# Copying the diagonal blocks of a 64x64 triangular inverse on GpSimd instead of ScalarE, in a one-core RWKV-7 / RetNet inference step

## The chip, the core and the metric

The kernel runs on one core of a Trainium2 chip. The metric is the device time of one execution in microseconds (us); the number that counts is the median of several runs. The profile comes from one more execution of the same program.

The engines are called here as the profile calls them: PE (TensorE, matmuls; PEld is its weight load), DVE (VectorE), ACT (ScalarE), POOL (GpSimd) and SP (which only issues transfers). Each engine works through its own list of instructions strictly in order, so an instruction that waits holds back everything behind it on that engine.

## What is computed

The reference is one step of a two-layer decoder over 256 prompt tokens and 8 single-token samples, which the kernel treats as one matrix of 264 columns. Layer 0 mixes with RWKV-7, layer 1 with RetNet; each layer has a gated feed-forward block ahead of and behind its mixer. The change lies in RWKV-7:

```python
def step(S, inp):                      # one token, per head; S is 64 x 64
    r_t, d_t, k_t, v_t, kk_t, a_t = inp
    sa = jnp.einsum('bhvk,bhk->bhv', S, -kk_t)
    S = (S * d_t[:, :, None, :] + sa[..., None] * (kk_t * a_t)[:, :, None, :]
         + v_t[..., None] * k_t[:, :, None, :])
    return S, jnp.einsum('bhvk,bhk->bhv', S, r_t)
```

## The kernel before

The 256 prompt tokens are taken in four chunks of 64, for 16 heads, two heads to a group of 128 partitions (`f` = 0 to 7). Inside a chunk the recurrence is a unit lower triangular system of 64x64 for each head and chunk. `inverse()` inverts all 64 of them at once, in blocks of 32: DVE inverts the diagonal blocks by back substitution (62 short operations `tm<-V,A` and `V<-V,tm`), transposes them into `Xd` (which lies in `tm`) and transposes half of them again into `AT`. The diagonal blocks are then copied to their places in the result `X`, and the off-diagonal block comes from two rounds of 32x32 matmuls, `ps<-tm,AT` and `ps<-V,AT`, each in two halves with an ACT copy out of PSUM between.

What uses `X` is `heads2(p)`, p = 0 to 3, for two groups each. In its order on PE: `al,ka` and `pp,ka`; `PI,be` and `pp,be` (DVE then takes `M` out of PSUM); `cst,al`; `PI,ka` and `cst,vt` (needs the value rows `vt` of its groups); `VK,KQ`; `z,X` and `aT,X` (needs `X`); `bT,WT` and `M,WT`; a long run of `VK`, `WT,bT`, `KQ,VK`, `M,WT` (called the sums below); three times `G,Ls` and `Ly,G`, with a DVE addition `G<-ps,G` after each; then the head norm `Y,cst`, `sq,cst`, `rd,cst`. `decode()` treats the 8 samples beside it: two times `dS,kkr` on states `dS` that POOL loads, each followed by an ACT copy `yd<-ps` and a matmul `cst,yd`.

The main line of work beside these is the value projection: 8 matmuls `ps<-xv,raw` for each `f`, after which ACT takes the value row out (`vt<-ps`, in `values`). These `xv` matmuls are PE's filler between the short matmuls. Their weights are read straight from the transfer's buffer `raw`. Behind them come the weights of the gate and of the output projection, which are split in two parts instead: ACT writes `hi` from `raw` (L90) and DVE writes `lo` from both (L105), which frees the buffer. There are three `raw` buffers in all, and SP loads the next unit into a buffer as soon as it is free.

The order of instructions is not written by hand. `weave` runs the main line and the side generators against a planner's clock: each operation that goes through a helper (`self.act`, `self.tt`, `self.mm`) adds its planned cost to its engine's clock by `spent`, and side work is let in when the clock says that its inputs are ready. An instruction recorded directly on `nc.gpsimd` adds nothing. Every matmul has line L138, every activation L90, most DVE operations L105.

Of the kernel before, what the change touches and what calls it, by code (L numbers as in the profile page):

```python
# [41 lines left out]
class Step:  # L42
# [158 lines left out]
    def mark(self, key):  # L201
        self.done[key] = self.now
# [242 lines left out]
class Rwkv(Step):  # L445
# [19 lines left out]
    def rwkv(self, gain):  # L465
        nc, tc, ps_, late = self.nc, self.tc, self.ps, self.late
# [5 lines left out]
        with ExitStack() as ctx:  # L472
# [33 lines left out]
            X = P1.tile([128, 32, 64], F32, name="X")  # L506
# [33 lines left out]
            def stream():  # L540
# [26 lines left out]
                for g in range(2):  # L567
                    kp = [ps_()[:, 0:T] for _ in range(4)]
                    for k in range(KT):
                        yield f"mix{k}"  # L570
                        for j in range(4):
                            prod(kp[j], "k", k, 4 * g + j)
                            yield
                    k_out(g, kp)
                self.beside(TU["inverse"], inverse())
                def vs(f):
                    p = ps_()[:, 0:T]
# [219 lines left out]
            def inverse():  # L797
                V, tm = (big(n).rearrange("p (a b) -> p a b", b=32) for n in ("V", "tm"))
                flat32 = lambda t: t.rearrange("p a b -> p (a b)")
                nc.gpsimd.memset(V, 0.0)  # L800
                nc.gpsimd.memset(flat32(V)[:, 0:1024:33], 1.0)
                for f in range(KT):
                    yield f"A{f}"
                self.turn(A3.rearrange("p r s -> p s r"), Ag)
                for m in range(31, 0, -1):
                    n = 32 - m
                    o = tm[:, 0:n, 0:m]
                    self.tt(o, V[:, m:32, m:m + 1].to_broadcast([128, n, m]),
                            A3[:, m:m + 1, 0:m].to_broadcast([128, n, m]))
                    self.tt(V[:, m:32, 0:m], V[:, m:32, 0:m], o, ALU.add)  # L810
                    if TU["INVY"] and m % TU["INVY"] == 0:
                        yield

                Xd = tm
                self.turn(Xd.rearrange("p n i -> p i n"), V)
                mark("W0")
                for e0 in EH:
                    self.turn(AT[e0:e0 + 32], Xd[e0:e0 + 32])
                for e0 in EH:
                    self.act(X[e0 + 32:e0 + 64, :, 32:64], Xd[e0 + 32:e0 + 64])  # L820
                    self.act(X[e0:e0 + 32, :, 0:32], Xd[e0:e0 + 32])
                yield
                for g in range(2):
                    py = ps_().rearrange("p (n s) -> p n s", n=16)
                    for n in range(16):
                        for e0 in EH:
                            hi = slice(e0 + 32, e0 + 64)
                            self.mm(py[e0:e0 + 32, n], AT[hi, 16 * g + n], Xd[hi, 16 * g + n])
                    for e0 in EH:
                        self.act(V[e0:e0 + 32, 16 * g:16 * g + 16], py[e0:e0 + 32])  # L830
                    yield
                for g in range(2):
                    px = ps_().rearrange("p (n s) -> p n s", n=16)
                    for n in range(16):
                        for e0 in EH:
                            lo = slice(e0, e0 + 32)
                            self.mm(px[lo, n], AT[lo, 16 * g + n], V[lo, 16 * g + n])
                    for e0 in EH:
                        self.act(X[e0:e0 + 32, 16 * g:16 * g + 16, 32:64], px[e0:e0 + 32])
                    mark(f"X{g}")  # L840
                    yield
# [758 lines left out]
```

## Time and profile before

| | us |
|---|---|
| three timed runs | 1284.57, 1288.61 (median), 1290.11 |
| the profiled execution | 1283.95 |
| its span, first to last instruction | 1282.2 |
| busy in it: PE, DVE, ACT, POOL | 1254.6, 849.4, 674.1, 68.8 |

The span and 1.75 us around it make the profiled execution's time. PE is busy for 98% of the span, so the time changes when PE is made to wait more or less, and not by what another engine saves for itself. The stretch that the change touches lies at 300 to 420 us.

### The profile page before, as it was taken

How to read it: one execution, taken by the hardware profiler on the slowest of the kernel's cores; microseconds unless marked ns; L12 is line 12 of the kernel's file. 1: busy time of each engine (PE TensorE's matmuls, PEld its weight loads, DVE VectorE, ACT ScalarE, POOL GpSimd, SP SyncE). 2: the span in 40 equal slices, each digit the busy share in tenths (PEclk: the TensorE clock that was granted, in tenths of full speed). 3: DMA queues.
4: the chain of work that ended last, by engine and by line, in shares of the span. 5: the costliest groups of instructions: out<-in, count | busy, mean ns of one | idle time of the engine just before them, and what ended most of it. 6: DMA issues, size and time to landing. Idle time of an engine off the chain costs nothing.

```text
span 1282.2 us, 29100 instructions
## 1 busy us (share of the span) xinstructions
PE 1254.6 (98%) x12194; PEld 1184.4 (92%) x12194; DVE 849.4 (66%) x1391; ACT 674.1 (53%) x1169; POOL 68.8 (5%) x175
## 2 busy tenths in 40 slices
PE   9999999999988999999999999999999999999996
PEld 9999998678777999999999999988888799999996
DVE  6766567589246877766566656677877865766554
ACT  7544442653444777754456454445665554544542
POOL 0000001131200000000000000011111100000000
PEclk9999999999999999999999999999999999999998
DMA  7655554333401566665557555679879655555562
GB/s 236 196 181 181 180 167 140 100 101 117 158 14 43 182 215 216 213 198 181 180 196 264 181 181 181 203 255 348 306 254 329 224 181 180 175 181 180 179 182 83
DMA packets 66755, 239.16 MB, mean 187 GB/s; under 512 B 7504, under 2 KB 8912, under 8 KB 66496
## 3 DMA queue, kind: packets, MB, share of 16 engines
q1 hardware_dynamic: 59472, 212.63, 51.8%
q0 software_dynamic: 6544, 23.40, 4.9%
q8 instruction: 95, 1.56, 0.5%
q10 hardware_dynamic: 608, 1.28, 0.3%
q14 instruction: 36, 0.29, 0.1%
HBM read 214.92 MB, written 22.35 MB: 185 GB/s over the span
## 4 chain that ended last, share of the span: by engine, by line
PE 87%; issue 5%; DMA 3%; DVE 2%; ACT 2%; SPq 0%; DVEq 0%; POOL 0%; ACTq 0%; POOLq 0%
PE ps L138 86%; DMA raw<-in_w 2%; PE ps L153 1%; DVE lo L105 1%; ACT hi L90 1%; DMA dS<-in_wkvt 1%; DMA Sd<-in_wkv 0%; DMA S<-in_ret 0%; ACT L90 0%; DMA out_swkv<-Sd 0%; DVE yl L105 0%; DVE xf L105 0%; DVE on L120 0%; DVE rs L126 0%; ACT sd L90 0%
## 5 line engine op out<-in xcount | busy, mean ns | idle before, releaser
L90 ACT ACTIVATE hi<-raw 128x1024 fp32r<-128x1024 f32 (+1 forms) x344 | 362.6, 1054 | 428.3 <-PE ps L138 210.4
L105 DVE TENSOR_TENSOR lo<-raw,hi 128x1024 fp32r<-128x1024 f32 (+1 forms) x344 | 418.5, 1217 | 229.6 <-ACT hi L90 228.1
L138 PE MATMUL ps<-ah,hi 128*128 128x264 f32 (+1 forms) x1824 | 522.0, 288 | 0.9 <-ACT ah L90 0.8
L138 PE MATMUL ps<-al,hi 128*128 128x264 f32 (+1 forms) x1824 | 515.8, 284 | 0.0
L138 PE MATMUL ps<-ah,lo 128*128 128x264 f32 (+1 forms) x1824 | 513.3, 284 | 0.1
L138 PEld LDWEIGHTS ps<-ah,hi 128*128 128x128 f32 x1824 | 342.0, 188 | 9.2 <-issue 7.4
L138 PEld LDWEIGHTS ps<-al,hi 128*128 128x128 f32 x1824 | 342.7, 188 | 4.1 <-issue 2.9
L138 PEld LDWEIGHTS ps<-ah,lo 128*128 128x128 f32 x1824 | 341.5, 188 | 0.5 <-DVE lo L105 0.3
L138 PE MATMUL ps<-hh,hi 128*128 128x264 f32 x832 | 237.1, 285 | 0.0
L138 PE MATMUL ps<-hl,hi 128*128 128x264 f32 x832 | 237.0, 285 | 0.0
L138 PE MATMUL ps<-hh,lo 128*128 128x264 f32 x832 | 236.8, 285 | 0.0
L138 PEld LDWEIGHTS ps<-hl,hi 128*128 128x128 f32 x832 | 156.8, 188 | 0.0
L138 PEld LDWEIGHTS ps<-hh,lo 128*128 128x128 f32 x832 | 156.7, 188 | 0.0
L138 PEld LDWEIGHTS ps<-hh,hi 128*128 128x128 f32 x832 | 156.4, 188 | 0.1
L105 DVE TENSOR_TENSOR h<-s,ps 128x264 f32<-128x264 f32 x88 | 37.0, 427 | 48.0 <-PE ps L138 46.6
L105 DVE TENSOR_TENSOR t<-ps,rs 128x264 f32<-128x264 f32 x88 | 37.2, 430 | 18.9 <-PE ps L138 18.8
L114 DVE SCALAR_TENSOR_TENSOR S<-ps,ks,S 128x512 f32<-128x512 f32 x64 | 45.0, 742 | 6.2 <-PE ps L138 6.2
L90 ACT ACTIVATE S<-S 128x1024 f32<-128x1024 f32 x32 | 33.7, 1056 | 16.1 <-DMA S<-in_ret 15.9
L90 ACT ACTIVATE hh<-h 128x264 fp32r<-128x264 f32 x88 | 35.3, 409 | 5.8 <-DVE h L105 5.5
L90 ACT ACTIVATE s<-t 128x264 f32<-128x264 f32 x88 | 35.3, 410 | 4.2 <-DVE t L105 4.1
L105 DVE TENSOR_TENSOR hl<-h,hh 128x264 fp32r<-128x264 f32 x88 | 37.0, 427 | 0.4
L90 ACT ACT_TABLE_LOAD x26 | 33.4, 1283 | 2.1 <-PEq L1580 1.7
(265 smaller groups left out, 1196.3 us busy)
## 6 DMA issues: line engine op xcount, KB each, us to landing
raw<-in_w SPq DMA_DIRECT2D x363, 512.0 KB, 3.7
S<-in_ret SPq DMA_DIRECT2D x32, 512.0 KB, 6.1
out_sret<-S POOLq DMA_DIRECT2D x32, 512.0 KB, 3.9
dS<-in_wkvt POOLq DMA_DIRECT2D x4, 512.0 KB, 5.4
Sd<-in_wkv SPq DMA_DIRECT2D x4, 512.0 KB, 5.7
out_swkv<-Sd POOLq DMA_DIRECT2D x4, 512.0 KB, 4.4
out_pret<-so POOLq DMA_DIRECT2D x8, 256.0 KB, 2.3
rcst<-in_rcst SPq DMA_DIRECT2D x1, 1100.0 KB, 6.2
```

What stands on the lines that cost most here:

```text
L90: ins = self.nc.scalar.activation(out=out, in_=in_, func=func, scale=scale, **kw)
L105: ins = self.nc.vector.tensor_tensor(out=out, in0=a, in1=b, op=op)
L114: ins = self.nc.vector.scalar_tensor_tensor(out=out, in0=a, scalar=s, in1=b, op0=op0, op1=op1)
L138: ins = self.nc.tensor.matmul(out=out, lhsT=lhsT, rhs=rhs, start=start, stop=stop)
L153: self.nc.tensor.transpose(out, in_, ident)
```

## The change

Four instructions move from ACT to POOL: the copies of the inverse's diagonal blocks from `Xd` into `X`.

```diff
                 for e0 in EH:
-                    self.act(X[e0 + 32:e0 + 64, :, 32:64], Xd[e0 + 32:e0 + 64])
-                    self.act(X[e0:e0 + 32, :, 0:32], Xd[e0:e0 + 32])
+                    nc.gpsimd.tensor_copy(X[e0 + 32:e0 + 64, :, 32:64], Xd[e0 + 32:e0 + 64])
+                    nc.gpsimd.tensor_copy(X[e0:e0 + 32, :, 0:32], Xd[e0:e0 + 32])
                 yield
```

The copies no longer go through `self.act`, so the planner's ACT clock does not count them, and the order of the whole stretch behind them comes out otherwise. On POOL the four copies stand ahead of the first load of `dS`; up to the place shown next, all engines have the same order as before, but for one exchange of short DVE operations. SP's list is the same. What SP's loads wait for is not.

PE, from about 305 us on (the operands are those named above; `x24` counts equal matmuls in a row; - is before, + is after):

```order
 L138 MATMUL ps<-cst,al 64x64 x24
-L138 MATMUL ps<-xv,raw 128x264 x25
-L138 MATMUL ps<-tm,AT 32x32 x32
-L138 MATMUL ps<-xv,raw 128x264
+L138 MATMUL ps<-xv,raw 128x264 x5
 L138 MATMUL ps<-PI,ka 64x64 x16
 L138 MATMUL ps<-cst,vt 64x64 x16
+L138 MATMUL ps<-xv,raw 128x264 x11
+L138 MATMUL ps<-VK,KQ 64x64 x16
+L138 MATMUL ps<-tm,AT 32x32 x32
+L138 MATMUL ps<-xv,raw 128x264 x3
+L138 MATMUL ps<-tm,AT 32x32 x32
```

Before, 25 `xv` matmuls stand ahead of the inverse's first round; now 16 do, and the first pair of groups has its `PI,ka`, `cst,vt` and `VK,KQ` ahead of it. From `cst,al` to the first `cst,yd` PE has 48 `xv` matmuls before the change and 37 after it, with the same short matmuls; the other 11 now stand later.

ACT, from the first split of a weight unit to the first `yd<-ps` (before):

```order
L90 ACTIVATE hi<-raw 128x1024
L90 ACTIVATE vt<-ps 128x264
L90 ACTIVATE WT<-ps 128x448 x2
L90 ACTIVATE hi<-raw 128x1024
L90 ACTIVATE X<-ps 32x16x32 x2
L90 ACTIVATE hi<-raw 128x1024
L90 ACTIVATE G<-ps 128x256 x2
L90 ACTIVATE Y<-ps 128x256 x2
L90 ACTIVATE yd<-ps 128x64
```

and the same place after:

```order
L90 ACTIVATE hi<-raw 128x1024
L90 ACTIVATE G<-ps 128x256 x2
L90 ACTIVATE Y<-ps 128x256 x2
L90 ACTIVATE hi<-raw 128x1024 x2
L90 ACTIVATE yd<-ps 128x64
```

The second and third `hi` moved behind `G` and `Y`, directly ahead of `yd`. DVE has it alike: its three `lo<-raw,hi` stood apart, ahead of `Ls` and `Ly`; now the three stand together behind `Ls` and `Ly` and directly ahead of the first `G<-ps,G`.

SP, the loads of weights with buffer numbers and the semaphores that each waits for: raw_4300 and the two ahead of it hold `xv` weights, the next three are split (before):

```order
L159 DMA raw_4211<-in_w 128x1024 [waits DMAHW5_49,PE_49]
L159 DMA raw_4300<-in_w 128x1024 [waits DMAHW6_49,PE_49]
L159 DMA raw_4590<-in_w 128x1024 [waits DMAHW7_49,PE_49]
L159 DMA raw_5160<-in_w 128x1024 [waits DMAHW0_49,PE_49]
L159 DMA raw_5509<-in_w 128x1024 [waits DMAHW2_49,DVE_49]
```

and after, where raw_4329 and raw_4799 are the last two units of `xv` weights:

```order
L159 DMA raw_4329<-in_w 128x1024 [waits DMAHW5_49,PE_49]
L159 DMA raw_4799<-in_w 128x1024 [waits DMAHW6_49,PE_49]
L159 DMA raw_5095<-in_w 128x1024 [waits DMAHW7_49,PE_49]
L159 DMA raw_5445<-in_w 128x1024 [waits DMAHW2_49,DVE_49]
L159 DMA raw_5543<-in_w 128x1024 [waits DMAHW3_49,DVE_49]
```

A wait for PE is a wait for the last `xv` matmul on a buffer, a wait for DVE one for a `lo` that frees it. Before, two buffers come free from `xv` matmuls for the units to be split (raw_4590, raw_5160). After, only one does (raw_5095, after the `xv` matmul behind `M,WT`); raw_4329 and raw_4799 keep the other two until `xv` matmuls that stand behind the first `cst,yd`, and so raw_5445 and raw_5543 each wait for the `lo` of the unit ahead of them.

## Rows read from the trace of the kernel before

**Rows 1.** The page: busy time of each engine, its share of the span, its instructions.

```profile
PE 1254.6 (98%) x12194; PEld 1184.4 (92%) x12194; DVE 849.4 (66%) x1391; ACT 674.1 (53%) x1169; POOL 68.8 (5%) x175
```

**Rows 2.** Busy time in stretches of the touched part: length, then busy us (and instructions) of PE, PEld, DVE, ACT and POOL, granted clock, DMA share, GB/s.

```profile
305.00:320.00 15.00, 14.96 (x213) 12.46 (x212) 14.42 (x36) 6.26 (x13) 1.32 (x2) 1.00 0.47 141
320.00:340.00 20.00, 19.95 (x519) 15.92 (x514) 4.82 (x8) 12.65 (x24) 2.83 (x7) 1.00 0.45 146
340.00:350.00 10.00, 7.22 (x314) 6.22 (x308) 1.82 (x7) 1.88 (x7) 3.75 (x9) 0.83 0.41 116
350.00:360.00 10.00, 8.41 (x316) 6.75 (x306) 3.99 (x12) 1.92 (x6) 0.99 (x2) 1.00 0.34 131
360.00:370.00 10.00, 8.89 (x363) 7.47 (x360) 3.40 (x12) 6.51 (x19) 0.00 (x0) 1.00 0.03 5
370.00:380.00 10.00, 9.18 (x265) 7.52 (x259) 6.05 (x19) 4.11 (x15) 0.00 (x0) 1.00 0.02 4
380.00:390.00 10.00, 9.46 (x318) 8.45 (x313) 3.93 (x13) 5.29 (x16) 0.00 (x0) 1.00 0.02 5
390.00:400.00 10.00, 9.19 (x193) 7.33 (x186) 6.81 (x22) 3.51 (x8) 0.00 (x0) 1.00 0.17 54
```

**Rows 3.** The same view in stretches of 1 us, with the same columns.

```profile
343.00:344.00 1.00, 0.20 (x11) 0.04 (x2) 0.00 (x0) 0.00 (x0) 0.00 (x0) 1.00 0.34 131
346.00:347.00 1.00, 1.00 (x7) 0.54 (x6) 0.00 (x0) 0.22 (x1) 0.75 (x1) 0.67 0.00 0
347.00:348.00 1.00, 1.00 (x13) 0.70 (x14) 0.00 (x0) 0.39 (x1) 1.00 (x3) 0.50 0.06 16
348.00:349.00 1.00, 1.00 (x42) 1.00 (x44) 0.36 (x2) 0.00 (x0) 1.00 (x4) 0.50 0.65 82
349.00:350.00 1.00, 1.00 (x56) 1.00 (x52) 0.00 (x0) 0.05 (x1) 1.00 (x4) 0.62 0.85 233
```

**Rows 4.** The view of the DMA queues, from 343 to 344 us: packets, MB, share of 16 engines. Queue q8 brings instructions.

```profile
q8 instruction: 1, 0.02, 5.6%
```

**Rows 5.** PE's waits from 280 to 470 us: what was waited for, us in total, times, longest.

```profile
PE ps L138 <- issue: 4.9, 5, 2.8
PE ps L138 <- DVE rd L105: 2.6, 2, 1.6
PE ps L138 <- DMA dS<-in_wkvt: 0.8, 1, 0.8
PE ps L138 <- ACT sq L90: 0.5, 1, 0.5
```

**Rows 6.** PE's timeline: start, busy us, engine, line, operation, tiles, shapes, count (a matmul of f32 is two instructions), and in brackets the idle time before it with what ended it.

```profile
305.37 11.39 PE L138 MATMUL ps<-xv,raw 128*128 128x264 f32 x50
...
331.83 0.69 PE L138 MATMUL ps<-z,X 64*64 64x64 f32 x32
...
336.78 2.49 PE L138 MATMUL ps<-xv,raw 128*128 128x264 f32 x10
...
345.98 0.31 PE L138 MATMUL ps<-dS,kkr 64*32 64x64 f32 x5 [2.78 <-issue]
...
350.76 0.34 PE L138 MATMUL ps<-cst,yd 128*64 128x64 f32 x4
```

**Rows 7.** DVE's timeline, same columns.

```profile
307.87 0.42 DVE L105 TENSOR_TENSOR M<-ps,cst 128x256 f32<-128x256 f32 x1
308.41 0.42 DVE L105 TENSOR_TENSOR M<-ps,cst 128x256 f32<-128x256 f32 x1
...
311.67 1.97 DVE L132 STREAM_TRANSPOSE tm<-V 128x1024 f32<-128x1024 f32 x1
...
331.69 1.23 DVE L105 TENSOR_TENSOR lo<-raw,hi 128x1024 fp32r<-128x1024 f32 x1 [10.81 <-ACT hi L90]
...
348.12 0.36 DVE L105 TENSOR_TENSOR G<-ps,G 128x64 f32<-128x64 f32 x2 [6.65 <-PE ps L138]
```

**Rows 8.** ACT's timeline, same columns.

```profile
313.68 4.25 ACT L90 ACTIVATE X<-tm 32x1024 f32<-32x1024 f32 x4 [12.86 <-DVE tm L132]
...
330.60 1.06 ACT L90 ACTIVATE hi<-raw 128x1024 fp32r<-128x1024 f32 x1 [1.20 <-DMA raw<-in_w]
...
335.64 1.06 ACT L90 ACTIVATE hi<-raw 128x1024 fp32r<-128x1024 f32 x1 [1.75 <-DMA raw<-in_w]
...
346.33 0.22 ACT L90 ACTIVATE yd<-ps 128x64 f32<-128x64 f32 x1 [3.79 <-PE ps L138]
```

**Rows 9.** The tile `raw` from 325 to 345 us: time from a load's issue to its landing.

```profile
DMA to landing us min/median/max: 3.5/4.2/5.1
```

**Rows 10.** POOL's groups of instructions over the whole span: line, engine, operation, tiles, shapes, count | busy us, mean ns of one | idle before.

```profile
L110 POOL TENSOR_TENSOR PI<-cst,PL 128x256 f32<-128x256 f32 x8 | 5.2, 677 | 11.1 <-PE ps L138 11.1
L508 POOL MEMSET X<- 32x1024 f32 x2 | 1.9, 945 | 0.1
L110 POOL TENSOR_TENSOR xf<-xf,rs 128x264 f32<-128x264 f32 x2 | 1.8, 922 | 251.0 <-DVE rs L126 251.0
```

**Rows 11.** Timelines of DVE and of POOL around 291 us, columns as in rows 6.

```profile
290.64 0.40 DVE L105 TENSOR_TENSOR tm<-V,A 128x231 f32<-128x231 f32 x1
291.08 0.87 DVE L105 TENSOR_TENSOR V<-V,tm 128x231 f32<-128x231 f32 x1
...
291.07 2.84 POOL L110 TENSOR_TENSOR PI<-cst,PL 128x256 f32<-128x256 f32 x4 [11.09 <-PE ps L138]
```

## The prediction, made before the changed kernel was run

> **What bounds the kernel now.** I read three views, in this order. The page first: PE is busy for 1254.6 us of 1282.2, POOL for 68.8 [rows 1]. A microsecond that ACT saves is worth nothing by itself; the time changes by what PE stands idle, or runs at a lower clock. The stretches next: ahead of 340 us PE hardly stands still (14.96 of 15, 19.95 of 20), although ACT is blocked there for 12.86 us at `X<-tm` [rows 8]: 25 `xv` matmuls in a row, 11.39 us, fill PE meanwhile [rows 6]. Behind 340 us PE does lose time: 2.78 us from 340 to 350, then 1.59, 1.11, 0.82, 0.54 and 0.81 in the next five tens [rows 2], 7.65 in all. PE's waits and its timeline say on what: 2.78 on its own instructions, "issue", ahead of 345.98, when one packet of the instruction queue comes in [rows 3, 4], the rest on `rd`, on `dS`, on issue again [rows 5, 6]. Behind the stop of 2.78 the granted clock is 0.67, 0.50, 0.50 and 0.62 of full in the four stretches that begin at 346, 347, 348 and 349 us, of which 0.50 is 1.2 GHz; that is 0.33 + 0.50 + 0.50 + 0.38 = 1.7 us of work not done, with the edges some 1.8 [rows 3]. So the stretch costs PE 7.65 + 1.8 = 9.45 us now. PE's matmuls stay the same ones, so the change is worth 9.45 less the same sum of the kernel after.
>
> **What it removes.** ACT loses four copies, 4.25 us, and a wait of 12.86 us, behind which the value rows stood [rows 8]. The wait cost PE nothing, as `xv` matmuls covered it. They are a fixed stock, though: after, five of them stand where 25 stood, and 11 are kept for behind `cst,yd`. Eleven at 11.39 / 25 = 0.456 us are 5.0 us of filler for the holes of 350 to 400 us. That is the gain to be had: I take it that holes on `rd`, `dS`, `sq` that now cost 0.5 to 1.5 us each shrink to 1.0 in all (0.5 to 1.5). Issue stalls do not go by filler. Of the 4.9 us of them the 2.78 may fall into the wait described below, where it costs nothing more; of the other 2.1 I keep half, 1.1 (0 to 2.1) [rows 5].
>
> **What it adds on POOL.** A copy of 32x1024 f32 from SBUF is not in the trace. The nearest rows: writing the same shape, 0.945 us; 256 elements a partition with two inputs, 0.677, or 2.7 us for 1024; 264 with two inputs, 0.922, or 3.6 us [rows 10]. I take 2.7 as the value: a copy reads what it writes, which the 0.945 leaves out, and `PI` is the nearest row that reads. The copies start when DVE's transpose has landed, at 313.68, and end at 313.68 + 4 x 0.945 = 317.5, 324.5 or 328.1. `z,X` wants them at 331.83 less 14 `xv` matmuls that no longer stand ahead (6.4), plus 1.2 (next part): 326.6. So they cost nothing up to 2.7 us each, and 1.5 at 3.6; the loads of `dS` behind them on POOL start later by as much. No gain comes from POOL itself. Beside it, in the trace: while POOL's `PI` ran (four, 2.84 us) a DVE product of two inputs, 0.40 just before, took 0.87 [rows 11]. The Trainium skill, "SBUF — State Buffer", section "SBUF: two separate sides", says why: a port pair that DVE and GpSimd share is locked for a whole instruction, and a DVE operation with two SBUF inputs blocks against a GpSimd operation that reads SBUF. It speaks against the change; the trace agrees (0.87 for 0.40); by it alone the sum here would stay, since DVE has nothing urgent in its 10.81 us of idle time behind the transposes [rows 7].
>
> **What it moves, small.** After, `PI,ka` of the first pair comes 5 x 0.456 us behind 305.37, at 307.65. It needs the PSUM banks that DVE frees with `M`; the second `M` ends at 308.41 + 0.42 = 308.83 [rows 7]. PE waits 1.2 us there.
>
> **What it moves, large.** This decides. `cst,yd` needs `yd`, which ACT writes behind three `hi`; each `hi` needs a load. Before, the loads had landed in turn (ACT waited 1.20 and 1.75 us for two of them, [rows 8]) and PE found `yd` ready but for its own stall. After, two of three buffers keep `xv` weights until behind `cst,yd`, and the third serves three units in a row, each waiting for the `lo` of the one ahead.
> - When does it come free? `z,X` at 326.6; from there to the `xv` behind `M,WT` it took 336.78 - 331.83 = 4.95 us, plus three more `xv` now (1.4), plus that matmul (0.46): 333.4.
> - The chain: load 4.2 (3.5 to 5.1, [rows 9]), `hi` 1.06, `lo` 1.23 [rows 7, 8], load, `hi`, `lo`, load, `hi`: 3 x 4.2 + 3 x 1.06 + 2 x 1.23 = 18.2 us, so 351.6, and with `yd` (0.22) 351.8.
> - When does PE arrive? From 305.37 to 350.76 it took 45.4 us before [rows 6]. Less 48 `xv` (21.9), the stall (2.78) and the slow clock (1.8), 18.9 are left; with 37 `xv` (16.9) and the 1.2: 305.37 + 16.9 + 18.9 + 1.2 = 342.4.
> - PE waits 351.8 - 342.4 = 9.4 us. Behind it the third `lo` ends at 351.6 + 1.23, and `G<-ps,G` (0.36) is late for the next `G,Ls` by 0.7. In all 10.1; with loads of 3.5 us 8.0, of 5.1 us 12.8.
> The stop is longer than the one that halved the clock before, so I charge the same 1.8 behind it (0 to 1.8). ACT holds `vt` and DVE holds `G` behind the chain, and PE's followers of both.
>
> **Sum.** After: 1.2 + 10.1 + 1.8 + 1.0 + 1.1 = 15.2; before 9.45; 5.7 us slower. On the profiled execution, 1283.95, that is 1289.7. It lies 4.7 us under the median of the three runs, 1288.61; the mean of all four is 1286.8, and I put the forecast at 1286.8 + 5.7 = **1292.5**. 0.5% is 6.4 us here, about what a measurement can tell from no change.
>
> The Trainium skill, "Runtime: NRT & Kernel Launch", section "Instruction fetch mechanics", has the fetch of the next 256 instructions mostly hidden, where the row shows 2.78 us unhidden; by it the 1.1 would be nothing and the time 1291.4.
>
> **The rivals.**
> - *Given back exactly.* Loads land at the short end, 3.5 us, in a quiet stretch, half of the slow clock or none: 1.2 + 8.0 + 1.0 + 0.5 = 10.7 against 9.45, +1.3: 1288. For it: with one buffer in use few loads run beside each other. Against: the `dS` loads fall in the same stretch (share 0.85 at 349 us, [rows 3]).
> - *More.* The loads meet those of `dS` at 5.1 us, all of the other issue stalls stay, small waits 1.5: 1.2 + 12.8 + 1.8 + 1.5 + 2.1 = 19.4, +10: 1297. POOL at 3.6 us a copy adds 1.5 at `z,X`, and the chain starts as much later, twice the harm in all: 1300.
> - *Faster.* The chain costs nothing, because the buffer comes free earlier than I count: if two of the three loads can be issued before PE's last `xv`, `yd` waits only for what ACT has at hand. It decides from 333.4 - 9.4 = 324.0 on: free by then, `cst,yd` has no wait. Then 1.2 + 0.8 + 1.0 + 1.1 = 4.1 against 9.45, 5.3 faster: 1281.5. For it: the stock of filler is real, and before, ACT was blocked for 12.86 us. Against: the order of loads and readers, which leaves one buffer.
> - *Nothing, since PE's order is what it was* is excluded by the order shown.
>
> **How the numbers follow.** Forecast 0.46 (its own range 1288 to 1296), given back 0.20, more 0.25, faster 0.09. Of the forecast's 0.46 0.27 is within 0.5% and 0.19 slower; of given back 0.18 within and 0.02 faster; of more 0.06 within and 0.19 slower; of faster 0.08 faster, 0.01 within. That makes faster 0.10, same 0.52, slower 0.38. The range from 1284 to 1300 leaves out most of the faster case, and the far end of more, some 2 in 10.
>
> **What would show it.** ACT: no 12.86 us at `X<-tm`, and instead 3 to 5 us on the load of `raw` three times between 333 and 352 us. PE: about 1.2 us on DVE's `M` near 308, a wait of 8 to 13 us for ACT's `yd` near 342, granted clock 0.5 behind it, and holes of under 0.5 us from 360 to 400. POOL: four copies of 1 to 2.7 us ended by 326. I am wrong if loads of `raw` start well ahead of 333, if the holes behind 360 us stay as they are, or if `X` is late at `z,X`.

## The result

The changed kernel took 1294.9 us in the median (1293.40 to 1301.23), the kernel before on the same chip 1289.14: a ratio of 1.0059 with a 95% interval of 1.0037 to 1.0081. That is 5.8 us slower by the medians and 7.6 by the ratio (4.8 to 10.4). Measured once more on another occasion (below) the ratio was 1.0067, from 1.0048 to 1.0086. The forecast was 1292.5, 5.7 us slower, with a range of 1284 to 1300. So the sign was right, and the size too by the medians; by the ratio it was a little short. One of the runs below, of hold3_no_ds, took 1431.48 us at a granted clock of 0.805 and is counted in no median and no ratio.

The profiled execution took 1294.62 us, its span 1292.2. That is 10.7 us more than the profiled execution of the kernel before: 6.3 of them lie in the touched stretch (below), and 3.3 in two pieces at half clock, near 421 and 1022 us, of which the last section tells. In this execution the rows look like this.

The page, busy time of each engine, against [rows 1]: POOL has gained 3.7 us of work, ACT has lost 4.2, and PE is busy for 3.9 us more in a span that is 10.0 us longer.

```profile
PE 1258.5 (97%) x12194; PEld 1186.2 (92%) x12194; DVE 850.9 (66%) x1391; ACT 669.9 (52%) x1165; POOL 72.5 (6%) x179
```

The stretches of [rows 2], columns as there:

```profile
305.00:320.00 15.00, 14.31 (x294) 11.74 (x292) 14.39 (x32) 4.81 (x12) 5.32 (x7) 1.00 0.34 107
320.00:340.00 20.00, 19.84 (x623) 16.22 (x623) 4.79 (x15) 8.22 (x16) 2.70 (x6) 1.00 0.37 109
340.00:350.00 10.00, 3.34 (x138) 2.72 (x138) 2.33 (x2) 2.00 (x5) 2.41 (x5) 0.79 0.59 188
350.00:360.00 10.00, 7.48 (x164) 5.17 (x168) 5.33 (x15) 2.70 (x6) 0.00 (x0) 0.70 0.24 78
360.00:370.00 10.00, 8.79 (x260) 7.18 (x249) 2.60 (x8) 5.13 (x13) 1.53 (x3) 1.00 0.19 57
370.00:380.00 10.00, 10.00 (x375) 8.21 (x377) 3.49 (x11) 3.13 (x9) 0.19 (x1) 1.00 0.10 18
380.00:390.00 10.00, 8.59 (x268) 6.67 (x261) 4.36 (x15) 4.78 (x15) 0.00 (x0) 1.00 0.11 43
390.00:400.00 10.00, 9.67 (x280) 8.05 (x273) 6.21 (x20) 4.91 (x17) 0.00 (x0) 1.00 0.02 5
```

From 340 to 360 us PE now stands still for 9.2 us where it stood 4.4; from 360 to 400 it stands for 2.95 where it stood 3.28. The filler that was kept did fill the holes of 370 to 380, and others opened beside them. PE's own timeline says on what it stood, columns as in [rows 6]:

```profile
308.77 0.33 PE L138 MATMUL ps<-PI,ka 64*64 64x64 f32 x4 [0.48 <-DVE M L105]
309.31 0.62 PE L138 MATMUL ps<-PI,ka 64*64 64x64 f32 x26 [0.21 <-DVE M L105]
...
333.56 2.49 PE L138 MATMUL ps<-xv,raw 128*128 128x264 f32 x10
...
352.52 0.48 PE L138 MATMUL ps<-cst,yd 128*64 128x64 f32 x4 [9.04 <-ACT yd L90]
...
367.52 0.62 PE L138 MATMUL ps<-PI,ka 64*64 64x64 f32 x26 [1.21 <-DVE Ly L105]
...
383.87 0.38 PE L138 MATMUL ps<-cst,vt 64*64 64x64 f32 x9 [0.68 <-issue]
385.73 0.32 PE L138 MATMUL ps<-sq,cst 128*32 128x64 f32 x8 [0.41 <-ACT sq L90]
388.56 1.13 PE L138 MATMUL ps<-rd,cst 128*128 128x256 f32 x4 [0.32 <-DVE rd L105]
```

ACT's timeline shows the chain, one `hi` after another, each waiting for its load, and `yd` behind the third:

```profile
338.79 1.06 ACT L90 ACTIVATE hi<-raw 128x1024 fp32r<-128x1024 f32 x1 [4.09 <-DMA raw<-in_w]
...
345.31 1.06 ACT L90 ACTIVATE hi<-raw 128x1024 fp32r<-128x1024 f32 x1 [4.37 <-DMA raw<-in_w]
351.30 1.06 ACT L90 ACTIVATE hi<-raw 128x1024 fp32r<-128x1024 f32 x1 [4.93 <-DMA raw<-in_w]
352.26 0.21 ACT L90 ACTIVATE yd<-ps 128x64 f32<-128x64 f32 x1
```

And the stretches of 1 us in and behind the stop, columns as in [rows 3]: the granted clock is 0.50 (1.2 GHz) in the middle of the stop, and still so for the first 3.5 us in which PE works again.

```profile
346.00:347.00 1.00, 0.00 (x0) 0.00 (x0) 0.60 (x1) 0.37 (x1) 0.00 (x0) 0.50 0.89 352
...
352.00:353.00 1.00, 0.48 (x5) 0.36 (x5) 0.61 (x1) 1.00 (x4) 0.00 (x0) 0.50 0.00 0
353.00:354.00 1.00, 1.00 (x2) 0.43 (x2) 1.00 (x4) 0.34 (x1) 0.00 (x0) 0.50 0.00 0
354.00:355.00 1.00, 1.00 (x17) 0.89 (x16) 1.00 (x3) 0.00 (x0) 0.00 (x0) 0.50 0.52 66
355.00:356.00 1.00, 1.00 (x8) 0.54 (x4) 0.34 (x3) 0.00 (x0) 0.00 (x0) 0.50 0.75 262
356.00:357.00 1.00, 1.00 (x53) 0.77 (x56) 0.43 (x1) 0.00 (x0) 0.00 (x0) 0.97 0.49 197
```

POOL's timeline has the copies, each for itself:

```profile
314.22 1.03 POOL L820 COPY X<-tm 32x1024 f32<-32x1024 f32 x1 [13.43 <-DVE tm L132]
...
317.46 1.14 POOL L821 COPY X<-tm 32x1024 f32<-32x1024 f32 x1
```

They take 1.03 to 1.14 us each, ACT took 4.25 for four. They are done at 318.60, and `z,X` comes at 327.

### The profile page after: what moved, and what is told of

Read it like the earlier page. It is cut to its first block, busy times and chain, and to the rows that moved or that the text cites. A ratio compares the mean times of both kernels' runs of the same rounds, so it can differ in the third digit from the quotient of the medians.

```text
span 1292.2 us, 29107 instructions
## 1 busy us (share of the span) xinstructions
PE 1258.5 (97%) x12194; PEld 1186.2 (92%) x12194; DVE 850.9 (66%) x1391; ACT 669.9 (52%) x1165; POOL 72.5 (6%) x179
## 4 chain that ended last, share of the span: by engine, by line
PE 90%; DVE 4%; DMA 2%; ACT 2%; issue 1%; SPq 0%; DVEq 0%; ACTq 0%
PE ps L138 89%; DMA raw<-in_w 1%; PE ps L153 1%; DVE V L105 1%; DVE tm L105 1%; ACT hi L90 1%; DVE lo L105 1%; DMA rcst<-in_rcst 1%; DMA S<-in_ret 0%; ACT L90 0%; DVE KQ L105 0%; DVE xf L105 0%; ACT yl L90 0%; ACT sd L90 0%; DVE sd L126 0%
## 5 line engine op out<-in xcount | busy, mean ns | idle before, releaser
L138 PE MATMUL ps<-part,hi 128*128 128x264 f32 (+1 forms) x176 | 34.8, 309 | 0.0
```

Of the source, the lines that this page charges most:

```text
L138: ins = self.nc.tensor.matmul(out=out, lhsT=lhsT, rhs=rhs, start=start, stop=stop)
```

## The experiments

The theory from the prediction: the move to POOL costs nothing, and the loss comes from the order that the planner makes once its ACT clock no longer counts the copies; in it one buffer serves three loads in a row ahead of `yd`, and PE stops. The first rival is that the copies on POOL cost something themselves; the second that PE stops at the first `cst,yd` for something else, and `yd` is only the last to come. All ratios are to the kernel before on the same chip.

### The engine alone: pool_planned

```diff
-                    self.act(X[e0 + 32:e0 + 64, :, 32:64], Xd[e0 + 32:e0 + 64])
+                    nc.gpsimd.tensor_copy(X[e0 + 32:e0 + 64, :, 32:64], Xd[e0 + 32:e0 + 64])
+                    self.spent("act", 0.05 + 0.000836 * 1024, X[e0 + 32:e0 + 64, :, 32:64], Xd[e0 + 32:e0 + 64])
...
```

> The four copies run on GpSimd, but the planner is still charged for them as if they ran on ACT, so that every engine keeps the order of the kernel before. My theory (the loss comes from the new order, not from the engine): four copies of 1.0 to 1.1 us each on POOL from about 313.7, X ready by 318.5, no wait of 12.9 us on ACT, PE as idle from 340 to 400 us as before (7 to 8 us), time 1288 to 1290, ratio to before 0.998 to 1.002. Rival (copies on POOL cost something themselves, by holding up DVE or by X being late): PE idle grows by 3 us or more near 318 to 332 and the time is above 1292.

Measured: 1286.02 us against 1286.86, ratio 0.9990 (0.9979 to 1.0002). The engine costs nothing, and gives nothing that can be told from nothing, although ACT no longer waits 12.9 us. PE has the stop of the kernel before at the same place, on its own timeline:

```profile
345.45 0.43 PE L138 MATMUL ps<-dS,kkr 64*32 64x64 f32 x5 [2.85 <-issue]
```

The first rival falls.

### The order alone: act_unplanned

```diff
-                    nc.gpsimd.tensor_copy(X[e0 + 32:e0 + 64, :, 32:64], Xd[e0 + 32:e0 + 64])
+                    nc.scalar.activation(out=X[e0 + 32:e0 + 64, :, 32:64], in_=Xd[e0 + 32:e0 + 64], func=AF.Copy)
...
```

> The order of the changed kernel on every engine, but the four copies on ACT again (they stand there ahead of the second value row). My theory (order and engine are two things): the chain is still there, PE stops at the first cst,yd for 8 to 10 us, and ACT, which cannot begin the copies before DVE's transpose at 314 us and then needs 4.25 us, holds the value row that cst,vt of the first pair wants at 309.8 until 318.8: another 9 us, so about 1304, 1306 with the slow clock behind it. Rival (the engine is what costs): with the copies back on ACT the time goes back to 1289.

Measured: 1306.95 us, ratio 1.0148 (1.0129 to 1.0166). PE's timeline has both waits, at the value row and at `yd`:

```profile
319.72 1.12 PE L138 MATMUL ps<-cst,vt 64*64 64x64 f32 x28 [8.76 <-ACT vt L90]
...
367.80 0.48 PE L138 MATMUL ps<-cst,yd 128*64 128x64 f32 x4 [8.24 <-ACT yd L90]
```

So engine and order can be read apart: before's order does not care where the copies run (1.000 and 0.999), the new order needs them off ACT (1.006 on POOL, 1.015 on ACT), and is the slower one with either.

### The chain, shortened by one: hold_third

The splits of chosen weight units are pinned to their place in program order, behind the last `xv` matmul; here the third one alone (`held()` takes one entry off the list's end for each unit that is split).

```diff
-            self.act(hi[:, s], raw[:, s])
-            self.tt(lo[:, s], raw[:, s], hi[:, s], ALU.subtract)
+            h = self.act(hi[:, s], raw[:, s]); self.pinned = self.held()
+            self.pinned and self.tc.keep_in_program_order(h); self.tt(lo[:, s], raw[:, s], hi[:, s], ALU.subtract)
...
+                self.hold = [True, False, False]; g2.extend(self.wt("rw_g2", 0, f) for f in range(KT))
```

> The changed kernel, with the split of the third weight unit pinned to its place in program order, which is behind the first yd: two hi instead of three stand ahead of yd on ACT, two lo instead of three ahead of G on DVE. My theory (PE's stop is a chain of load, hi, lo through one buffer): the second hi ends at about 346.4 as it does in the changed kernel, yd at 346.6, PE waits 3.1 us at the first cst,yd in place of 9.0; the time falls by 5.9, to about 1289.0, or to 1287.2 if the clock then stays up. Rival (PE stops there for something else, the loads of dS or its own instructions, and yd is only the last to come): the stop stays at 8 us or more, and the time at 1293 to 1296.

Measured: 1289.72 us, ratio 1.0020 (1.0006 to 1.0034). PE's timeline:

```profile
327.70 0.32 PE L138 MATMUL ps<-V,AT 32*32 32x32 f32 x4 [1.88 <-issue]
...
351.98 0.34 PE L138 MATMUL ps<-cst,yd 128*64 128x64 f32 x4 [2.06 <-ACT yd L90]
354.28 0.62 PE L138 MATMUL ps<-xv,raw 128*128 128x264 f32 x1 [1.54 <-issue]
```

One link less takes 7.0 us off the wait for `yd` (9.04 to 2.06; 5.9 expected, and PE itself came late here after a stop of 1.88), and some 5 us off the time by the ratios (1.0059 to 1.0020), where 5.9 were forecast. The second rival falls. But right behind it stands a new stop of 1.54 on PE's own instructions.

### No chain: hold3

As above with `self.hold = [True] * 3`.

> The changed kernel, with the splits of the first three weight units pinned behind the last xv matmuls: no hi stands ahead of yd, no lo ahead of G. My theory: no wait for yd over 0.5 us, 9.0 us less idle time and up to 1.8 us less slow clock, so 1294.9 - 9.0 - 1.8 = 1284.1; if the stop on PE's own instructions of the kernel before (2.8 us, and the slow clock behind it 1.8) comes back, 1288.7. The splits are then later, and PE may wait for part,hi near 385 to 400 us, which would cost 1 to 4 us. Rival (the stop has another cause): 1293 to 1296, with the stop of about 9 us at the same place.

Measured: 1290.34 us, ratio 1.0026 (1.0013 to 1.0038). The wait for `yd` is gone, and the time isn't where it should be. PE's timeline shows what stands there instead:

```profile
325.84 0.25 PE L138 MATMUL ps<-V,AT 32*32 32x32 f32 x4 [1.33 <-issue]
...
348.86 0.49 PE L138 MATMUL ps<-xv,raw 128*128 128x264 f32 x1 [2.57 <-issue]
```

The stop on instructions that the kernel before had in `dS,kkr` is back, 2.57 us of it, right behind `cst,yd`. In the changed kernel it fell into the nine microseconds of the stop (its packet began at 345.58) and cost nothing more. The time came out 1.6 us above the worse of the two that I had named, and some 4 us above it when both are taken against the kernel before, which was 2.3 us faster on this chip (1286.86 against 1289.14).

### Is it the pins? hold3_before

The same pins in the kernel before.

> The kernel before (copies on ACT, its order) with the same three splits pinned behind the last xv matmuls. There the hi did not hold up yd, so nothing is to be gained. If holding the splits back costs something by itself (PE waits for part,hi or part,lo at 370 to 400 us), the time is 1 to 3 us above before, and that much of hold3's 3.4 us belongs to the pins and not to the new order. If it costs nothing, the ratio is 0.999 to 1.001, and the whole 3.4 us belong to the new order.

Measured: 1286.72 us, ratio 0.9998 (0.9986 to 1.0010). In the old order the pins cost nothing in all, so I put what hold3 is slower by, 3.4 us, down to the new order. The profile shows two changes that offset each other in part. PE waits 1.13 us for `hi` at 377.71, and the stop ahead of `dS,kkr`, 2.78 us in the kernel before, is down to 1.31, with the granted clock at 1.00 behind it:

```profile
345.23 0.30 PE L138 MATMUL ps<-dS,kkr 64*32 64x64 f32 x4 [1.31 <-issue]
```

In the kernel before, loads of `raw` are in flight ahead of this place; here the pinned splits keep the buffers, and from 339 to 347 us the queues move 16 GB/s at most.

### Does filler cure the stops on instructions? hold3_spread and hold3_spread2

```diff
+                    if p == 0 and q == 0: yield 1.0
...
+                        if h == 0 and n == 7: yield 1.0
```

The first line stands between the halves of the sums, the second in the middle of the first `dS,kkr`; both are of hold3_spread. hold3_spread2 has a `yield 0.0` instead behind both halves of every pair's sums, and in the middle and at the end of each `dS,kkr`.

> As hold3 (no hi ahead of yd), and two yields more, in the middle of the first sums and of the first dS,kkr, so that xv matmuls stand between the short ones: 5, then half the sums, 1, half of dS,kkr, 1, the other sums, the other dS,kkr, 3. My theory (what is left of the loss in hold3 is mostly PE's stops on its own instructions, 5.7 us from 280 to 470, which the stop for yd had covered in the changed kernel and which come where short matmuls stand together without filler): those stops fall to 3.5 us or less, none above 1.5 us between 340 and 352, and the time by 2 to 4 us against hold3, to 1286 to 1288. Rival (these stops do not go by filler): 5 to 6 us of them as before, time 1289 to 1291.

> Another spread of the same xv matmuls on hold3: yields after both halves of every pair's sums and in the middle and at the end of both dS,kkr. First stretch: 5, half the sums, 1, the other half and half of dS,kkr together, 1, the rest of dS,kkr, 2. My theory: between the two others, since half the sums and half of dS,kkr stand together without filler; stops on PE's own instructions of 3 to 5 us, time 1287 to 1289. Rival (filler is no matter): as hold3, 1290.

Measured: 1302.73 us, ratio 1.0123 (1.0105 to 1.0140), and 1294.39, ratio 1.0055 (1.0036 to 1.0075). Both miss by far, in the wrong direction, so this theory fell. What cost hold3_spread2 its time was not followed up. PE's timeline of the first:

```profile
354.82 0.38 PE L138 MATMUL ps<-pp,ka 64*64 64x64 f32 x4 [4.82 <-issue]
```

Stretches of 1 us from there, columns as in [rows 3]; what to see is the DMA share, last but one, and the rate behind it:

```profile
350.00:351.00 1.00, 0.00 (x0) 0.00 (x0) 0.69 (x1) 0.09 (x1) 0.00 (x0) 1.00 1.01 332
351.00:352.00 1.00, 0.00 (x0) 0.00 (x0) 0.00 (x0) 0.00 (x0) 0.00 (x0) 1.00 1.01 348
352.00:353.00 1.00, 0.00 (x0) 0.00 (x0) 0.00 (x0) 0.00 (x0) 0.00 (x0) 1.00 0.99 393
353.00:354.00 1.00, 0.00 (x0) 0.00 (x0) 0.00 (x0) 0.00 (x0) 0.00 (x0) 1.00 0.25 86
```

The queues were full until 353, and the packet of PE's instructions began between 352 and 353, at the end of the burst of data. In hold3 it is the same: the queues are at their fullest in the stretch in which the packet begins, and PE goes on some 2 us behind that.

```profile
345.00:346.00 1.00, 1.00 (x45) 0.84 (x35) 0.38 (x1) 0.66 (x2) 0.00 (x0) 1.00 0.93 328
346.00:347.00 1.00, 0.28 (x1) 0.00 (x0) 0.90 (x2) 0.00 (x0) 0.00 (x0) 1.00 1.07 430
347.00:348.00 1.00, 0.00 (x0) 0.00 (x0) 0.00 (x0) 0.00 (x0) 0.00 (x0) 1.00 0.34 131
```

The DMA view of hold3 from 346 to 347 us, columns as in [rows 4]; a packet is counted where it begins, and 6.2% of 16 engines is 1.0 us of one:

```profile
q8 instruction: 1, 0.02, 6.2%
```

(In the first spread the two other kinds of new wait, 2.3 us for `z` and 2.6 for `hi`, add to it: another order is never another order at one place only.)

### The burst taken away: before_no_ds, hold3_no_ds, after_no_ds

```diff
-                    Ss = [load(2 * h + j) for j in range(2)]
+                    Ss = Ss if h else [load(2 * h + j) for j in range(2)]
```

These kernels leave out the second pair of state loads `dS`, 1 MB; the second `dS,kkr` reads the states of the first pair again.

> The kernel before without the second pair of state loads dS (1 MB on POOL's queue near 341 to 350 us); the second dS,kkr works on the first pair's states, so the samples' output is not the reference's. All engines keep their order. Theory (PE's stop on its own instructions comes where a packet of the instruction queue waits behind a burst of dS and raw): the stop of 2.8 us shrinks to under 1 us, the slow clock behind it goes, the wait for dS (0.8 to 1.5 us) goes too: 4 to 6 us less, about 1282 to 1283.5, ratio 0.995 to 0.997. Rival (the stop comes from the number of short matmuls alone): stop of 2.5 to 3 us as before, only the wait for dS is gained, 1286 to 1287.

> hold3 without the second pair of dS loads, as in the kernel beside it. Theory: the stop of 2.6 us at 346 to 349 us and the slow clock behind it go, 1290.3 - 4.4 = 1286, and what is left against the kernel beside it is the new order's own cost (waits for M 0.7 and Ly 1.2, stops on instructions of some 2 us at 320 to 327), 2 to 4 us. Rival: stop and time as in hold3.

> The changed kernel without the second pair of dS loads. My theory (the stop at the first cst,yd is the chain of load, hi, lo through one buffer, and dS has only a small part in how long its loads take): the stop stays at 7.5 to 9 us, 3.5 to 3.7 us for each load of raw, and the time falls by no more than 2 us, to 1293 to 1295. Rival (the dS loads slow the raw loads and so make the stop): the stop falls under 6 us and the time under 1291.

Measured: before_no_ds 1285.83 us, ratio 0.9977 (0.9968 to 0.9987), 1 to 3 us short of the gain expected; hold3_no_ds 1283.39, 0.9974 (0.9960 to 0.9987), 6.7 us under hold3 by the ratios, and level with before_no_ds where I had forecast 2 to 4 us more; after_no_ds 1293.75, 1.0055 (1.0038 to 1.0072), its stop at `yd` still 8.42 us. In hold3_no_ds PE's timeline has at the place in question

```profile
344.69 0.49 PE L138 MATMUL ps<-xv,raw 128*128 128x264 f32 x1 [0.65 <-issue]
```

and in before_no_ds, where I had forecast under 1 us,

```profile
348.00 0.40 PE L138 MATMUL ps<-dS,kkr 64*32 64x64 f32 x5 [2.52 <-issue]
```

as before. In that kernel the loads of `raw` run at this time, and they make a burst of their own (in hold3_no_ds the pinned splits keep the buffers, and there is none):

```profile
344.00:345.00 1.00, 1.00 (x87) 1.00 (x79) 0.00 (x0) 0.70 (x3) 0.00 (x0) 1.00 0.89 299
345.00:346.00 1.00, 0.48 (x31) 0.32 (x20) 0.00 (x0) 0.00 (x0) 0.00 (x0) 1.00 0.52 193
```

Its packet began between 345 and 346. So it is not `dS` as such: with either load in flight the packet came when the burst ended. My forecast for this kernel could not have come true, since in the kernel before POOL issues the second pair of `dS` only behind the stop, which ends at 345.98:

```profile
347.14 1.05 POOL L1048 DMA_DIRECT2D dS<-in_wkvt  x2
```

The nearest test for this order is hold3_before, where the loads of `raw` are the ones held back: 1.31 in place of 2.78.

### The same without leaving anything out: hold3_paced

```diff
+                        for c in range(4):
+                            for j in range(2):
+                                o = 1024 * (2 + j) + 256 * c
+                                pin(nc.gpsimd.dma_start(Ss[j][:, 4 * c:4 * c + 4], self.io["wkvt"][:, o:o + 256].rearrange("p (n v) -> p n v", v=64)))
+                                for _ in range(1 if (c, j) != (3, 1) else 0):
+                                    pin(nc.gpsimd.memset(pace, 0.0))
```

The slices also stand behind the two copies `kkr<-dq` on POOL, where hold3 has its loads ahead of them.

> hold3 with the second pair of dS loads cut into eight slices of 128 KB, with a short memset on POOL between them, so that 1 MB comes over 7 us instead of 3; all other engines keep hold3's order, and nothing is left out. Theory (a packet of PE's instructions waits behind whatever burst of data is in flight): without the burst the packet near 346 us lands in time, the stop of 2.6 us ahead of the first cst,yd falls under 1.2 us and the slow clock behind it goes; the slices may land late for the second dS,kkr, by up to 1 us: 1290.3 - 2.6 - 1.8 + 0.7 = 1286.6, ratio to before 0.998 to 1.0005. Rival (it was the work on dS itself, or the number of short matmuls): the stop stays at 2 to 3 us, ratio 1.002 to 1.004.

Measured: 1285.96 us against 1287.79, ratio 0.9988 (0.9977 to 0.9999). PE's timeline and two of its stretches:

```profile
344.81 0.49 PE L138 MATMUL ps<-xv,raw 128*128 128x264 f32 x1 [0.65 <-issue]
```

```profile
345.00:346.00 1.00, 1.00 (x18) 0.71 (x18) 0.28 (x2) 0.00 (x0) 1.00 (x3) 1.00 0.49 160
346.00:347.00 1.00, 1.00 (x35) 0.65 (x38) 0.49 (x2) 0.00 (x0) 1.00 (x4) 1.00 0.55 176
```

The same megabyte at 160 to 190 GB/s, a stop of 0.65 in place of 2.57, the clock at 1.00 from 305 to 410 us, and the ratio 1.0026 became 0.9988. This kernel keeps the copies on POOL and nothing is left out, with three splits pinned and two loads sliced, and it is a shade faster than the kernel before, though within 0.5%. Two cautions. hold3's other stop, 1.33 at 325.84, is missing from this profile too, and the slices have nothing to do with that one. And the packet for this place began at 342.41, ahead of the slices' data (from 342.85 on), while in hold3 the data came first (343.98, the packet at 346.66). Only the next packet met data at 160 to 190 GB/s: it began 4.00 us behind the one before, as in hold3_no_ds with quiet queues (4.05). So whether the slower rate or the later start of these loads took the stop away is not told apart.

### The changed kernel again: after_again

> The changed kernel once more, beside the others on one chip. Both theories: ratio to before 1.004 to 1.008, with the stop of about 9 us at the first cst,yd.

Measured: 1295.02 us, ratio 1.0067 (1.0048 to 1.0086). The wait for `yd` was 8.23. What the first profile did not have is this, on PE's timeline:

```profile
327.11 0.25 PE L138 MATMUL ps<-V,AT 32*32 32x32 f32 x4 [1.61 <-issue]
```

with another 0.80 at 321.75. Such stops at these two places of the order, 1.8 to 2.4 us together, stand in six of the ten profiles of kernels with the new order, and in none of the four with the old one, which have nothing there but a single 0.35. They come and go from one execution to the next.

## Why the prediction was right, and what was off

**The chain.** Free buffer at 333.4: 334.0 (333.56 and one matmul of `xv`, 0.46). Three links at 4.2 us a load: the three `hi` began 4.77 us behind the free buffer, then 4.2 and 3.7 us behind the `lo` ahead of them (1.23 us each behind their `hi`), 4.2 in the mean. `yd` at 351.8: 352.47. PE there at 342.4: 352.52 - 9.04 = 343.48. Wait 9.4: 9.04. The 0.7 for `G` was not seen; behind the stop PE ran at half clock, and PE did not wait for `G` there. Of the lengths forecast for the loads the middle one held, and hold_third shows the mechanism link by link.

**The slow clock.** 1.8 forecast; the rows above give 0.48 x 0.5 + 3 x 0.5 + 0.03 = 1.8. In the second profile of the changed kernel it was 2.5, above the bounds that I gave (0 to 1.8).

**The small terms.** `M`: 1.2 forecast, 0.48 + 0.21 = 0.7. Issue: 1.1, against 0.68 above and two of 0.16 and 0.20, 1.0. Small waits: 1.0, against 1.21 + 0.41 + 0.32 = 1.9; the 1.21 for `Ly` is a new wait that I had not named. Sum 0.7 + 9.0 + 1.8 + 1.0 + 1.9 = 14.4, forecast 15.2; less the 9.45 of before 5.0 against 5.7. That the sum came so near is in part luck: `M`, the wait for `yd` and `G` together were 1.6 us too much, the small waits 0.9 too little.

**Where it fell short.** From the `xv` matmuls behind `cst,al` to the last `rd,cst` the kernel before takes 413.12 - 305.37 = 107.75 us, the changed one 419.81 - 305.80 = 114.01 in its first profile, and 422.24 - 306.52 = 115.72 in the second: 6.3 and 8.0 us more. The term that was too small is the one for the stops on instructions. I took those that the kernel before has, and halved them, and gave the new order none of its own; in more than half of the profiles it has the ones at 320 to 328, 1.8 to 2.4 us. With them the 5.0 become 6.8 to 7.4, near the 7.6 and 8.6 us that the two ratios give. They are not all of it: the first profile has only 0.16 us of them, and of its 6.3 us 0.9 are busy time of PE (98.29 us against 97.42), for which the sum has no term; that rest stays open.

**POOL.** I took 2.7 us a copy, between 0.945 and 3.6; it was 1.03 to 1.14, next to the row that writes the same shape, so the nearest row by shape was the better one and not that with the nearest operands. The result does not hang on it. Four DVE operations with two SBUF inputs that ran beside the copies took 3.03 us, where the kernel before has 1.71 for the same four. The Trainium skill, "SBUF — State Buffer", section "SBUF: two separate sides", tells of a port pair that such an operation and a GpSimd operation that reads SBUF lock against each other; the trace agrees.

```profile
316.66 3.03 DVE L114 SCALAR_TENSOR_TENSOR rc<-rc,par,k 128x264 f32<-128x264 f32 x4
```

As forecast, that delay of 1.3 us went into DVE's idle time (7.93 us ahead of its next work from PE), and pool_planned, which has it too (3.03), loses nothing.

**The filler.** I had counted on the 11 `xv` matmuls to close PE's holes behind 360 us, to 1.0. They closed those on `dS` and most on `rd`, not those on `Ly` and on issue: 3.28 us of holes became 2.95. I had named it as a sign of being wrong that the holes behind 360 us stay as they are; they very nearly did, so this part of the mechanism was wrong, and its 1.0 should have been near 1.9. That an engine gets free work to do only helps if the work stands where the hole is.

## What to carry to other kernels

An edit that only moves four copies to an idle engine can still reorder everything behind it, if a planner counts what the edit takes away; compare the orders first, and keep the planner's cost where the order is to stay. In the new order look for buffers: count the units that must pass through each one ahead of an instruction that another engine waits for, and multiply by load plus use. And when a stop is taken away, ask which other stop it had covered: here 9 us of wait taken away gave some 4.5, because a stop on PE's own instructions stood behind it.

## What was not expected of the hardware

At PE's longest stops on its own instructions the packet that ended the stop began late in a burst of data or right behind it, and PE went on 2.2 to 2.4 us behind the packet's beginning: it stood still for 2.78 us in the kernel before, 2.57 in hold3, 4.82 in hold3_spread. In the kernel before the packet began between 343 and 344 us [rows 3, 4], and the stretch of 1 us ahead of it was

```profile
342.00:343.00 1.00, 1.00 (x83) 1.00 (x72) 0.00 (x0) 0.54 (x2) 0.00 (x0) 1.00 0.82 336
```

With the queues quiet ahead of the packet the stop was 1.31 in the old order (hold3_before) and 0.65 in the new one (hold3_no_ds). Short matmuls stand together at all of these places, but the filler that two runs put between them was no cure. The Trainium skill, "Runtime: NRT & Kernel Launch", section "Instruction fetch mechanics", has that fetch as mostly hidden; these rows measure where it isn't, and they decide.

The stops ahead of `V,AT` near 325 to 328 us, which come in some executions only, go the same way. One load of half a megabyte arrives there. In the four profiles of the new order without this stop the packet began ahead of the load's data (in hold3_no_ds at 321.56, the data from 321.68 on, a margin of 0.12 us); in the six with it the data came first, and the packet began in the load's last 0.6 us or at its end (in hold_third data from 322.88 to 325.33, the packet at 325.32, the stop 1.88). Why a packet comes behind the data, and at which moment PE asks for it, the traces do not show.

The same stop was also not always followed by the same clock. Ahead of the last `rd,cst`, at 410 to 420 us, both kernels stop for 0.5 us on `sq` and for 1.6 on `rd`; behind it the kernel before kept 1.00, and the changed kernel's first profile ran at 0.50:

```profile
421.00:422.00 1.00, 1.00 (x7) 1.00 (x6) 1.00 (x3) 0.05 (x1) 0.00 (x0) 0.50 0.00 0
```

for some 3.4 us, 1.7 us lost; its second profile kept 1.00 there. With the same wait, pool_planned and hold3_paced ran at half clock behind it, hold3 and hold_third did not. Another piece at half clock, 1.7 us lost from 1021 to 1025 us, is in the changed kernel's first profile, and not in its second or in that of the kernel before. Such pieces may be part of why executions of one kernel differ by several microseconds; they are not shown to be part of the change.
